# Centring a layer norm by two fp32r products on high and low parts, in place of one float32 product

## The chip, the cores and the metric

One core of a Trainium2 chip runs the whole program. The metric is the device time of one execution in microseconds (us). The kernel before takes 2686.6 us, the median of three runs (2685.15 to 2687.59).

## What is computed

One layer of a hybrid decoder trunk on 2048 tokens of width 1024, all in float32. After an RMS norm and one input projection, three groups of heads work side by side: a convolution module (A), a gated MLP with a spatial mix (B) and a state space model (C). Their outputs are concatenated, projected and added to the input; a squared-ReLU MLP and a final norm follow. The change concerns the layer norm over each head of 64 values, which A applies after its convolution and B to its gate:

```
def head_layernorm(x, g, b, n_heads):
    xf = x.astype(jnp.float32).reshape(*lead, n_heads, -1)
    mu = jnp.mean(xf, axis=-1, keepdims=True)
    xc = xf - mu
    var = jnp.mean(xc * xc, axis=-1, keepdims=True)
    y = (xc * lax.rsqrt(var + EPS)).reshape(*lead, -1)
    return y * g + b
...
ya: h = a_val * sigmoid(a_gate); h = causal_dwconv(h, conv_w, conv_b); h = head_layernorm(h, ln_g, ln_b, A_HEADS); silu(h)
yb: v = head_layernorm(gelu(v), ln_g, ln_b, B_HEADS); mix = einsum("hts,bcshp->bcthp", w, v) + b_s; gelu(u) * mix
```

## The kernel before

The tokens are done in two halves of 1024 (`h`), each in two blocks of 512 (`n`). The first stage, about the first 1010 us, holds input projection and mixers. `ORDER` lists the projection's column tiles of 128: a (A's gate and value), b (B's gate and input), x, z and d (C's), and s, where C's state space part begins. Large products take three fp32r products per tile: operands are split into a high and a low part (`split_w` for weights, `norm1_tr` for activations), and `mm3` (lines 247 to 249) adds high x high, high x low and low x high in one bank of PSUM.

The mixers' work is put between these products by a planner in the program. Each piece is a generator that yields the time at which it wants to go on; a clock per engine (`clk.pe`, `clk.dve`, `clk.act`, `clk.pool`) is advanced by estimates as instructions are written, and `pump`, called after every fourth step of a projection, runs the generators that are due. TensorE's order is the order of writing. The other engines are ordered by a list scheduler that knows priorities (`tc.high_priority`). Every engine runs its own queue strictly in order.

The layer norm is `centred_` (line 520). Channels lie on partitions, tokens on the free axis. For a tile of 128 channels x 512 tokens, four float32 products (line 525) multiply each 128x128 block, as the stationary operand, by the constant matrix `cen`: identity minus 1/64 within each head of 64. That transposes and centres at once, into one bank `pc` of the PSUM ring `ln`, which has two banks and also serves the transpositions `ta` and `tpx` and the spatial mix `pm`. Then ScalarE squares (line 528), VectorE sums over 64 (line 531), GpSimd takes the power -1/2 (`rstd_of`, lines 287 and 288), and VectorE multiplies `pc` by it (line 534), which frees the bank. A transposes the result back (`ta`, line 562); B multiplies it by the spatial weights (`pm`, line 617).

`gen_a` (line 538) runs once per half and a tile: 30 taps on VectorE (line 549, 1024 tokens), then `LAG_A1` = 12000 ns of the planner's time, then `centred` for each block. `gen_b` (line 610) runs once per half, b tile and block, behind the activation that makes the tile `gv` (two buffers). Both have 4 tiles x 2 halves x 2 blocks: 32 calls of `centred`.

The ring `raw` of four tiles of 128x512 (`RAWB`) takes loads of y for the output projection (`load_split`, line 274), which begins after the mixers.

Of the kernel before, what the change touches and what calls it, by code (L numbers as in the profile page):

```python
# [9 lines left out]
F32 = mybir.dt.float32  # L10
F32R = mybir.dt.float32r
# [5 lines left out]
P = 128  # L17
# [4 lines left out]
NB = T // 512  # L22
# [10 lines left out]
RAWB = 4  # L33

EVAC, PRI_S, PRI_L, PRI_X = 600, 60, 150, 300

LAG_S, LAG_A1, LAG_A2, LAG_B1, LAG_B2, LAG_N, LAG_DT, LAG_H = 3000, 12000, 5000, 1000, 5000, 5000, 20000, 4000
# [4 lines left out]
def kernel(  # L42
# [6 lines left out]
    nc = tc.nc  # L49
# [4 lines left out]
    def pool(stack, name, bufs=1, **kw):  # L54
        return stack.enter_context(tc.tile_pool(name=name, bufs=bufs, **kw))
# [9 lines left out]
    const = pool(ctx, "const")  # L65
# [3 lines left out]
    constm = pool(mixers, "constm")  # L69
# [28 lines left out]
    cen = constm.tile([P, P], F32, name="cen")  # L98
    nc.vector.tensor_copy(cen, ident)
    for j in range(2):  # L100
        js = slice(64 * j, 64 * j + 64)
        nc.vector.tensor_scalar_sub(cen[js, js], cen[js, js], 1.0 / 64)
    avg512 = constm.tile([P, 2], F32, name="avg512")
    nc.vector.memset(avg512, 1.0 / 512)
    caw = constm.tile([P, TAPS_A * 4], F32, name="caw")
# [76 lines left out]
    clk = Clk()  # L182
    gens = []

    def V(n, after=0.0):
        clk.dve = max(clk.dve, clk.pe, after) + n / 0.96 + 70
        return clk.dve

    def A(n, after=0.0):
        clk.act = max(clk.act, clk.pe, after) + n / 1.2 + 150  # L190
        return clk.act
# [93 lines left out]
    def rstd_of(ss, n, scale, eps_first=True):  # L285

        nc.gpsimd.tensor_scalar(ss, ss, scale, EPS, op0=ALU.mult, op1=ALU.add)
        nc.gpsimd.tensor_tensor(ss, ss, mhalf[:, 0:n], op=ALU.pow)
        clk.pool += n * 170
        return G(n)  # L290
# [211 lines left out]
    def proj(hT, w, n):  # L502
# [11 lines left out]
        mm3(pairs(), KT)  # L514
        return ps

    def centred(src, name):
        with tc.high_priority(offset=PRI_L):
            return centred_(src, name)

    def centred_(src, name):

        pc = psa.tile([P, 512], F32, tag="ln", name=f"pc_{name}")
        for i in range(4):
            nc.tensor.matmul(pc[:, i * P:(i + 1) * P], src[:, i * P:(i + 1) * P], cen, start=True, stop=True)
        clk.pe += 850
        sq = cv.tile([P, 512], F32, tag="sq", name=f"sq_{name}")
        nc.scalar.activation(sq, pc, AF.Square)
        t = A(512)
        v8 = cv.tile([P, 8], F32, tag="v8", name=f"v8_{name}")  # L530
        nc.vector.reduce_sum(v8, sq.rearrange("p (q e) -> p q e", e=64), axis=mybir.AxisListType.X)
        V(512, t)
        t = rstd_of(v8, 8, 1.0 / 64)
        nc.vector.tensor_mul(sq.rearrange("p (q e) -> p q e", e=64), pc.rearrange("p (q e) -> p q e", e=64),
                             v8.unsqueeze(2).to_broadcast([P, 8, 64]))
        V(512, t)
        return sq
# [3 lines left out]
    def gen_a(h, t, ht):  # L541
        while a_done[0] < 4 * h + t:
            yield clk.pe + 1000
        acc = cv.tile([P, T], F32, tag="aa", name=f"ca_{h}_{t}", bufs=1)
        nc.scalar.activation(acc, ht[:, 0:T], AF.Identity, scale=caw[:, t:t + 1],  # L545
                             bias=vecs[:, CAB + t:CAB + t + 1])
        A(T)
        for k in range(1, TAPS_A):
            nc.vector.scalar_tensor_tensor(acc, ht[:, k:k + T], caw[:, k * 4 + t:k * 4 + t + 1], acc,  # L549
                                           op0=ALU.mult, op1=ALU.add)  # L550
            V(T, clk.act if k == 1 else 0.0)
            if k % 2 == 0:
                yield clk.dve - 3000
        yield clk.dve + LAG_A1
        for n in range(NB):
            xn = centred(acc[:, n * 512:n * 512 + 512], f"a{h}{t}{n}")
            if n == NB - 1:
                a_done[0] += 1
            yield clk.dve + LAG_A2
            tp = psa.tile([P, 512], F32, tag="ln", name=f"ta_{h}_{t}_{n}")  # L560
            for i in range(4):
                nc.tensor.transpose(out=tp[:, i * P:(i + 1) * P], in_=xn[:, i * P:(i + 1) * P], identity=ident)
            clk.pe += 430
            yt = cv.tile([P, 512], F32, tag="yt", name=f"ya_{h}_{t}_{n}")
            nc.scalar.activation(yt, tp, AF.Silu, scale=vecs[:, LAG + t:LAG + t + 1],
                                 bias=vecs[:, LAB + t:LAB + t + 1])
            A(512)
            nc.gpsimd.dma_start(y_d[h][t * P:(t + 1) * P, n * 512:n * 512 + 512], yt)

    def seg_a(h, hT, t):  # L570
# [34 lines left out]
        if h + 1 < NHALF:  # L605
            nc.scalar.copy(halo_a[:, t, :], ht[:, T:T + TAPS_A - 1])
        finish([("u", 0)])
        spawn(gen_a(h, t, ht), ("a", h))

    def gen_b(h, t, n, gv, ug):  # L610
        yield clk.act + LAG_B1
        vn = centred(gv, f"b{h}{t}{n}")
        yield clk.dve + LAG_B2
        pm = psa.tile([P, 512], F32, tag="ln", name="pm")
        for i in range(4):
            for j in range(2):
                nc.tensor.matmul(pm[64 * j:64 * j + 64, i * P:(i + 1) * P],
                                 vn[:, i * P + 64 * j:i * P + 64 * j + 64], wsT[:, 2 * t + j, :],
                                 start=True, stop=True)
        clk.pe += 8 * 142  # L620
        yt = cv.tile([P, 512], F32, tag="yt", name=f"yb_{h}_{t}_{n}")
        nc.vector.scalar_tensor_tensor(yt.rearrange("p (i l) -> p i l", l=P), pm.rearrange("p (i l) -> p i l", l=P),
                                       vecs[:, LBG + t:LBG + t + 1],
                                       bsp[:, t, :].unsqueeze(1).to_broadcast([P, 4, P]),
                                       op0=ALU.mult, op1=ALU.add)
        nc.vector.tensor_mul(yt, yt, ug)
        V(1100)
        nc.gpsimd.dma_start(y_d[h][512 + t * P:512 + (t + 1) * P, n * 512:n * 512 + 512], yt)
# [137 lines left out]
    for h, order in enumerate(ORDER):  # L766
        for st_ in order.split():
            kind, t = st_[0], int(st_[1:])
# [319 lines left out]
    for bi, (h, kb) in enumerate(blocks):  # L1088
# [33 lines left out]
        for nq in range(4):  # L1122
# [11 lines left out]
            for c0 in range(0, NCH, 2):  # L1134
# [15 lines left out]
                acc = accs[h, c0, nq]  # L1150
# [7 lines left out]
                else:  # L1158
                    ps1 = psa.tile([P, 512], F32, tag="mm", name="mmo1")
                    for g, pg in enumerate((ps, ps1)):  # L1160
                        mm3([[(pg[:, j * NQ:(j + 1) * NQ],) + operands(4 * g + k, c0 + j) for j in range(2)]
                             for k in range(4)], 4)
                        for j in range(2):
                            c = c0 + j
# [76 lines left out]
    for n in range(len(seq1)):  # L1241
# [10 lines left out]
        i = n - (NP * NPAIR - LEADX)  # L1252
# [141 lines left out]
    for u in range(LASTP):  # L1394
        q, h, k = seq2[u]
# [9 lines left out]
        if k == 0 and q in (0, 1, 4):  # L1405
            pp, tag = (ps4[0], "mm2") if h else (ps3, "mm")
# [12 lines left out]
    for i, (u, c0) in enumerate(tail):  # L1419
# [4 lines left out]
        q, h, k = seq2[u]  # L1424
# [38 lines left out]
```

## Time and profile before

| what | value |
|---|---|
| median of three runs | 2686.6 us |
| the profiled execution | 2684.8 us, its span on the profile 2683.1 us |
| TensorE busy | 2640.4 us, 98% of the span |
| VectorE, ScalarE, GpSimd busy | 1738.6, 1325.8, 499.2 us |
| share of the span on the chain that ended last | TensorE 91%, DMA 3%, VectorE 2%, ScalarE, GpSimd and issue 1% each |
| TensorE's clock as granted | 0.997 of full over the run |

PE is TensorE and PEld its loads of stationary operands, which run beside products; DVE is VectorE, ACT ScalarE, POOL GpSimd, and SP the queue that issues most loads. The span is what the trace covers; the execution's own time is 1.7 us longer. A busy TensorE is not one at its peak. The views of the trace give, per group of instructions, count, busy time and mean duration, and the idle time before them with what ended it; the chain of waits goes back from the last instruction to whatever released each step.

### The profile page before, as it was taken

The page shows a single profiled execution, that of the slowest core. Times are in us where ns is not written, and L with a number is a line of the kernel's source. Part 1 is how long each engine was busy: PE and PEld are TensorE (multiplying, and loading weights), DVE is VectorE, ACT ScalarE, POOL GpSimd, SP SyncE. Part 2 cuts the span into 40 slices and gives each one's busy share as a digit, 9 for nine tenths or more (in the row PEclk, how much of TensorE's full clock was granted, in tenths as well). Part 3 has the DMA queues.
Part 4 walks back from the last instruction along what each step waited for, and adds up shares of the span by engine and source line. Part 5 has one row for each costly group of instructions (what it writes and reads, how often), then busy time and mean ns, then how long its engine had stood idle before and what let it go on. Part 6 is the DMA issues. An engine that isn't in the chain of part 4 may idle for free.

```text
span 2683.1 us, 38800 instructions
## 1 busy us (share of the span) xinstructions
PE 2640.4 (98%) x14018; PEld 2213.3 (82%) x14018; DVE 1738.6 (65%) x2641; ACT 1325.8 (49%) x2469; POOL 499.2 (19%) x628
## 2 busy tenths in 40 slices
PE   8999999999999999999998999999999999999998
PEld 6788887778878889999997788878887888888887
DVE  6787875496987844664437777787666433555434
ACT  5547673466676534543235455555545433333332
POOL 1013243123333321221052111111111000000001
PEclk9999999999999999999999999999999999999999
DMA  3343443234344226557388666686556645555543
GB/s 121 104 133 117 143 134 99 88 112 137 115 131 133 74 86 223 168 187 241 117 273 271 227 219 207 221 287 219 192 193 213 212 147 157 191 184 177 164 120 124
DMA packets 386897, 446.79 MB, mean 167 GB/s; under 512 B 28301, under 2 KB 279921, under 8 KB 386705
## 3 DMA queue, kind: packets, MB, share of 16 engines
q1 hardware_dynamic: 335520, 314.02, 38.6%
q0 software_dynamic: 28352, 96.62, 9.7%
q10 hardware_dynamic: 22832, 33.68, 3.5%
q8 instruction: 110, 1.80, 0.3%
q14 instruction: 83, 0.67, 0.1%
HBM read 297.28 MB, written 146.93 MB: 166 GB/s over the span
## 4 chain that ended last, share of the span: by engine, by line
PE 91%; DMA 3%; DVE 2%; ACT 1%; issue 1%; POOL 1%; SPq 0%; ACTq 0%; DVEq 0%; POOLq 0%
PE f L1050 14%; PE f L1048 14%; PE f L1049 14%; PE mm L247 10%; PE mm L248 10%; PE mm L249 10%; PE mmo L247 4%; PE mmo L249 4%; PE mmo L248 4%; PE yp L382 1%; PE sp L409 1%; PE op L372 1%; DMA raw_y<-y_d 1%; DMA raw_x<-t_d 1%; DMA raw_x<-h_d 1%
## 5 line engine op out<-in xcount | busy, mean ns | idle before, releaser
L1049 PE MATMUL f<-xlo,w1hi 128*128 128x512 f32 x896 | 352.7, 394 | 3.4 <-DVE xlo L992 3.4
L1048 PE MATMUL f<-xhi,w1hi 128*128 128x512 f32 x896 | 352.7, 394 | 3.0 <-DVE u L1207 3.0
L1050 PE MATMUL f<-xhi,w1lo 128*128 128x512 f32 x896 | 353.0, 394 | 2.6 <-DVE w1lo L1041 2.6
L975 DVE TENSOR_TENSOR falo<-fr,fahi 128x512 fp32r<-128x512 f32 (+1 forms) x237 | 155.3, 655 | 308.1 <-ACT fahi L974 287.7
L1048 PE MATMUL f<-wbhi,fahi 128*128 128x512 f32 x896 | 349.3, 390 | 3.9 <-ACT fahi L1289 3.9
L1050 PE MATMUL f<-wbhi,falo 128*128 128x512 f32 x896 | 349.4, 390 | 0.1
L1049 PE MATMUL f<-wblo,fahi 128*128 128x512 f32 x896 | 349.0, 390 | 0.0
L974 ACT CAST fahi<-fr 128x512 fp32r<-128x512 f32 (+1 forms) x237 | 140.3, 592 | 365.0 <-PE f L1049 360.2
L549 DVE SCALAR_TENSOR_TENSOR ca<-ht,caw,ca 128x1024 f32<-128x1024 f32 x240 | 316.3, 1318 | 5.8 <-ACT ca L545 2.6
L247 PE MATMUL mmo<-whi_o,hi_y 128*128 128x256 f32 x1024 | 294.1, 287 | 4.0 <-DVE x L1166 2.6
L249 PE MATMUL mmo<-whi_o,lo_y 128*128 128x256 f32 x1024 | 288.9, 282 | 0.4 <-DVE lo_y L266 0.4
L248 PE MATMUL mmo<-wlo_o,hi_y 128*128 128x256 f32 x1024 | 288.3, 282 | 0.0
L1050 PEld LDWEIGHTS f<-xhi,w1lo 128*128 128x128 f32 x896 | 169.2, 189 | 42.2 <-DVE w1lo L1041 4.4
L1049 PEld LDWEIGHTS f<-xlo,w1hi 128*128 128x128 f32 x896 | 169.2, 189 | 41.7 <-DVE xlo L992 4.0
L1048 PEld LDWEIGHTS f<-xhi,w1hi 128*128 128x128 f32 x896 | 169.2, 189 | 41.0 <-ACT w1hi L1040 3.4
L1048 PEld LDWEIGHTS f<-wbhi,fahi 128*128 128x128 f32 x896 | 168.6, 188 | 39.4 <-ACT fahi L1289 4.4
L247 PEld LDWEIGHTS mmo<-whi_o,hi_y 128*128 128x128 f32 x1024 | 193.0, 188 | 7.2 <-DVE x L1166 3.7
L1050 PEld LDWEIGHTS f<-wbhi,falo 128*128 128x128 f32 x896 | 168.5, 188 | 35.4 <-DVE falo L1290 0.4
L1049 PEld LDWEIGHTS f<-wblo,fahi 128*128 128x128 f32 x896 | 168.6, 188 | 35.1
L248 PEld LDWEIGHTS mmo<-wlo_o,hi_y 128*128 128x128 f32 x1024 | 193.2, 189 | 1.2 <-issue 1.2
L249 PEld LDWEIGHTS mmo<-whi_o,lo_y 128*128 128x128 f32 x1024 | 192.8, 188 | 0.7 <-DVE lo_y L266 0.6
L247 PE MATMUL mm<-hi_h,whi_x 128*128 128x512 f32 x384 | 159.0, 414 | 0.0
(313 smaller groups left out, 5515.2 us busy)
## 6 DMA issues: line engine op xcount, KB each, us to landing
fr<-f_d SPq DMA_DIRECT2D x208, 256.0 KB, 2.7
w<-in_w_ff_dram SPq DMA_DIRECT2D x176, 256.0 KB, 4.0
f_d<-fs POOLq DMA_DIRECT2D x96, 256.0 KB, 2.8
abc<-acs_d SPq DMA_DIRECT2D x32, 512.0 KB, 4.8
raw_y<-y_d SPq DMA_DIRECT2D x64, 256.0 KB, 4.5
wraw_o<-in_w_out_dram SPq DMA_DIRECT2D x64, 256.0 KB, 4.8
pr_w<-in_w_ff_dram SPq DMA_DIRECT2D x64, 256.0 KB, 5.0
w2t_d<-pr_w POOLq DMA_DIRECT2D x32, 512.0 KB, 4.3
```

The lines of the kernel that those rows point to most:

```text
L247: nc.tensor.matmul(ps, lh, rh, start=(i == 0 and j == 0), stop=False)
L248: nc.tensor.matmul(ps, lh, rl, start=False, stop=False)
L249: nc.tensor.matmul(ps, ll, rh, start=False, stop=(i == n - 1 and j == len(outs) - 1))
L372: nc.tensor.matmul(op[:, i * P:(i + 1) * P], prev[g][:, i * P:(i + 1) * P], xch[:, 5, :], start=True, stop=True)
L382: nc.tensor.matmul(yp[64 * j:64 * j + 64, i * P:(i + 1) * P], xdt[:, hh * 64:hh * 64 + 64], e_t[:, hh, :], start=True, stop=True)
L409: nc.tensor.matmul(sp, w["btok"], w["xdec"], start=True, stop=True)
L549: nc.vector.scalar_tensor_tensor(acc, ht[:, k:k + T], caw[:, k * 4 + t:k * 4 + t + 1], acc, op0=ALU.mult, op1=ALU.add)
L974: nc.scalar.copy(hi, raw)
L975: nc.vector.tensor_sub(lo, raw, hi.bitcast(F32))
L1048: nc.tensor.matmul(ps, lh, rh, start=start and i == 0, stop=False, skip_group_check=True)
L1049: nc.tensor.matmul(ps, lh, rl, start=False, stop=False, skip_group_check=True)
L1050: nc.tensor.matmul(ps, ll, rh, start=False, stop=last, skip_group_check=True)
```

## The change

`cen` is copied once into `cenr`, of type fp32r. A new generator step `cen_split` makes a high part (ScalarE's cast to fp32r) and a low part (VectorE's subtraction) of a 128x512 tile, in two buffers of the ring `raw`; a counter allows two splits that have not been centred yet. `centred_` then issues, for each of four blocks, two fp32r products into the same place of `pc`, one with the high part as the stationary operand and one with the low part. The planner's estimate for the products falls from 850 to 560 ns, and the split's cast and subtraction enter its clocks. A splits its first block behind the taps and its second right behind the first's centring; B splits `gv` as soon as it runs, and its lag counts from VectorE's clock in place of ScalarE's.

```diff
+    cenr = constm.tile([P, P], F32R, name="cenr")
+    nc.vector.tensor_copy(cenr, cen)
...
+    cq = [0]
+
+    def cen_split(src, name):
+
+        while cq[0] >= 2:
+            yield clk.pe + 500
+        cq[0] += 1
+        hi, lo = (const.tile([P, 512], F32R, tag="raw", name=f"c{i}_{name}", bufs=RAWB) for i in "hl")
+        with tc.high_priority(offset=PRI_L):
+            nc.scalar.copy(hi, src)
+            nc.vector.tensor_sub(lo, src, hi.bitcast(F32))
+        A(512)
+        V(512, clk.act)
+        return hi, lo
+
     def centred(src, name):
+        cq[0] -= 1
...
         for i in range(4):
-            nc.tensor.matmul(pc[:, i * P:(i + 1) * P], src[:, i * P:(i + 1) * P], cen, start=True, stop=True)
-        clk.pe += 850
+            for m in range(2):
+                nc.tensor.matmul(pc[:, i * P:(i + 1) * P], src[m][:, i * P:(i + 1) * P], cenr, start=m == 0,
+                                 stop=m == 1)
+        clk.pe += 560
...
+        parts = yield from cen_split(acc[:, 0:512], f"a{h}{t}0")
         yield clk.dve + LAG_A1
         for n in range(NB):
-            xn = centred(acc[:, n * 512:n * 512 + 512], f"a{h}{t}{n}")
+            xn = centred(parts, f"a{h}{t}{n}")
+            if n + 1 < NB:
+                parts = yield from cen_split(acc[:, 512:1024], f"a{h}{t}1")
...
     def gen_b(h, t, n, gv, ug):
-        yield clk.act + LAG_B1
-        vn = centred(gv, f"b{h}{t}{n}")
+        parts = yield from cen_split(gv, f"b{h}{t}{n}")
+        yield clk.dve + LAG_B1
+        vn = centred(parts, f"b{h}{t}{n}")
```

The new clocks move the pieces in every engine's order. Three places follow; a row has the line, the operation and output<-inputs, with the size of the output.

TensorE in the first half, where tile 3 of A (`pc_a`, `ta_3_0`) and tile 2 of B (`pc_b`) are centred, before:

```order
L562 MATMUL ta_3_0_3587<-ident,sq_a_3528 128x128 x4
L525 MATMUL pc_a_3595<-cen,ca_3_3010 128x128 x4
L247 MATMUL mm<-hi_h_4_386,whi_bu_3448 128x512
L248 MATMUL mm<-lo_h_4_387,whi_bu_3448 128x512
...
L249 MATMUL mm<-hi_h_7_413,wlo_bu_3449 128x512
L525 MATMUL pc_b_3619<-cen,gv_2_0_3496 128x128 x4
```

and now (`ch` and `cl` are the high and low parts):

```order
L585 MATMUL ta_3_0_3754<-ident,sq_a_3670 128x128 x4
L544 MATMUL pc_a_3762<-cenr,ch_a_3677 128x128
L544 MATMUL pc_a_3762<-cenr,cl_a_3678 128x128
...
L544 MATMUL pc_a_3762<-cenr,cl_a_3678 128x128
L544 MATMUL pc_b_3778<-cenr,ch_b_3738 128x128
L544 MATMUL pc_b_3778<-cenr,cl_b_3739 128x128
...
L249 MATMUL mm<-hi_h_0_352,whi_bv_3611 128x512
```

Each centring has eight products in place of four. A's second centring and B's next one had 12 projection products between them; now they are adjacent.

VectorE at the same place (`v` the sum of squares, `sq` the final multiply, `wlo` the low part of weights), before:

```order
L531 TENSOR_REDUCE v_a_3530<-sq_a_3528 128x8
L534 TENSOR_TENSOR sq_a_3528<-pc_a_3523,v_a_3530 128x512
L531 TENSOR_REDUCE v_a_3602<-sq_a_3600 128x8
L534 TENSOR_TENSOR sq_a_3600<-pc_a_3595,v_a_3602 128x512
L237 TENSOR_TENSOR wlo_bu_3634<-wraw_bu_0_3635,whi_bu_3633 128x512
L237 TENSOR_TENSOR wlo_bu_3634<-wraw_bu_4_3639,whi_bu_3633 128x512
L531 TENSOR_REDUCE v_b_3626<-sq_b_3624 128x8
L534 TENSOR_TENSOR sq_b_3624<-pc_b_3619,v_b_3626 128x512
```

and now:

```order
L529 TENSOR_TENSOR cl_b_3682<-gv_2_0_3569,ch_b_3681 128x512
L551 TENSOR_REDUCE v_a_3672<-sq_a_3670 128x8
L554 TENSOR_TENSOR sq_a_3670<-pc_a_3661,v_a_3672 128x512
L239 TENSOR_TENSOR wlo_bu_3700<-wraw_bu_0_3701,whi_bu_3699 128x512
L239 TENSOR_TENSOR wlo_bu_3700<-wraw_bu_4_3705,whi_bu_3699 128x512
L529 TENSOR_TENSOR cl_b_3739<-gv_2_1_3609,ch_b_3738 128x512
L551 TENSOR_REDUCE v_b_3733<-sq_b_3731 128x8
L554 TENSOR_TENSOR sq_b_3731<-pc_b_3722,v_b_3733 128x512
L551 TENSOR_REDUCE v_a_3773<-sq_a_3771 128x8
L529 TENSOR_TENSOR cl_b_3908<-gv_3_0_3794,ch_b_3907 128x512
L554 TENSOR_TENSOR sq_a_3771<-pc_a_3762,v_a_3773 128x512
```

A subtraction of a split stands ahead of a sum of squares twice, and once between a sum and its multiply.

SP's queue, which issues the loads: before, the first of four early loads of y stood among weight loads of the first half of the tokens:

```order
L235 DMA wraw_z_0_1262<-in_w_in_dram 128x4x128
L308 DMA abc_2_0_1778<-acs_d_63 128x1024
L274 DMA raw_y_8318<-y_d_57 128x512
L235 DMA wraw_z_4_1266<-in_w_in_dram 128x4x128
L235 DMA wraw_z_0_1339<-in_w_in_dram 128x4x128
```

and now the first loads of y stand at the end of the stage, with the output weights (`wraw_o`):

```order
L237 DMA wraw_z_4_8440<-in_w_in_dram 128x4x128
L878 DMA wraw_o_8650<-in_w_out_dram 128x2x256
L878 DMA wraw_o_8656<-in_w_out_dram 128x2x256
L276 DMA raw_y_8576<-y_d_57 128x512
L276 DMA raw_y_8582<-y_d_57 128x512
L878 DMA wraw_o_8674<-in_w_out_dram 128x2x256
```

All loads of y now follow the splits, which use the same ring.

## Rows read from the trace of the kernel before

**Rows 1.** The page: span, then busy us, share of span, instructions.

```profile
span 2683.1 us, 38800 instructions
...
PE 2640.4 (98%) x14018; PEld 2213.3 (82%) x14018; DVE 1738.6 (65%) x2641; ACT 1325.8 (49%) x2469; POOL 499.2 (19%) x628
```

**Rows 2.** TensorE's waits, 100 to 1010 us: total us, times, longest.

```profile
PE ta L562 <- DVE sq_a L534: 2.2, 2, 1.1
...
PE pc_b L525 <- DVE sq_a L534: 0.8, 1, 0.8
PE pm L617 <- ACT gv L638: 0.7, 1, 0.7
PE pc_b L525 <- DVE sq_b L534: 0.2, 1, 0.2
```

**Rows 3.** Line 525, B's products: count, ns min/median/max, first and last start.

```profile
L525 PE MATMUL pc_b<-cen,gv x128: 270/275/377, 374.1 to 993.4; 128*128 128x128 f32 x128
```

**Rows 4.** The chain of waits, start and us: first and last of six centrings, twice.

```profile
431.19 0.89 PE pc_a L525 x8
...
483.71 0.89 PE pc_b L525 x8
...
949.41 0.89 PE pc_a L525 x8
...
992.55 1.09 PE pc_b L525 x8
```

**Rows 5.** Timeline of products and loads: start, us, engine, line, count at the end.

```profile
84.83 1.85 PE L686 MATMUL td<-sel,dr 128*128 128x16 f32 x16
...
86.50 0.19 PEld L247 LDWEIGHTS mm<-hi_h,whi_x 128*128 128x128 f32 x1
...
86.61 0.19 PEld L248 LDWEIGHTS mm<-lo_h,whi_x 128*128 128x128 f32 x1
...
125.98 1.05 PE L525 MATMUL pc_a<-cen,ca 128*128 128x128 f32 x8
...
126.76 0.19 PEld L247 LDWEIGHTS mm<-hi_h,whi_x 128*128 128x128 f32 x1
```

**Rows 6.** Timeline of output projection's products, 256 columns: first and last of ten.

```profile
1030.05 0.28 PE L249 MATMUL mmo<-whi_o,lo_y 128*128 128x256 f32 x1
...
1031.11 0.28 PE L249 MATMUL mmo<-whi_o,lo_y 128*128 128x256 f32 x1
```

**Rows 7.** Groups by line: a weight split's cast and subtraction, busy us, mean ns.

```profile
L236 ACT CAST whi_z<-wraw_z 128x512 fp32r<-128x512 f32 x32 | 19.2, 617 | 26.5 <-PE mm L248 26.5
...
L237 DVE TENSOR_TENSOR wlo_z<-wraw_z,whi_z 128x512 fp32r<-128x512 f32 x32 | 21.2, 686 | 13.7 <-ACT whi_z L236 12.1 <-DMA xch<-xbc_d 1.7
```

**Rows 8.** Busy us by engine, sum over 100 to 1005 us in four stretches.

```profile
sum 905.00, PE 900.19 PEld 725.85 DVE 676.62 ACT 536.80 POOL 265.76; mean PE 225.05 PEld 181.46 DVE 169.15 ACT 134.20 POOL 66.44
```

**Rows 9.** The chain of waits at the four places where it leaves TensorE.

```profile
436.76 1.29 DVE wlo_bv L237 x2
...
446.77 0.83 ACT L646
...
452.92 1.13 PE pc_b L525 x8
...
746.75 0.62 ACT whi_x L236
...
960.02 0.91 PE pc_a L525 x8
...
964.67 0.70 DVE sq_a L534
```

**Rows 10.** Groups by line: activation-table loads.

```profile
L565 ACT ACT_TABLE_LOAD x14 | 18.0, 1283 | 2.9 <-PE ta L562 2.6
```

**Rows 11.** Loads of y: us to landing; first product on y.

```profile
raw_y<-y_d SPq DMA_DIRECT2D x64, 256.0 KB, 4.5
...
L247 PE MATMUL mmo<-whi_o,hi_y x1024: 278/282/682, 1011.4 to 1426.3; 128*128 128x256 f32 x171
```

## The prediction

> **What bounds the kernel now.** I read the page first: TensorE is busy for 2640.4 of 2683.1 us [rows 1]. Then the list of what TensorE waited for, in the stage that holds the layer norms (100 to 1010 us): four entries at the layer norms and behind them, 2.2 + 0.8 + 0.7 + 0.2 = 3.9 us in all [rows 2]. So TensorE's own work sets the time there, and the change can act in two ways only: by what it takes from or adds to TensorE's stream, or by making TensorE wait. Third, the instructions of line 525: 128 products for B [rows 3], and as many for A. The code has 16 calls of four products for each, so a float32 product is recorded as two, each with a load of its own: eight per call. In the chain of waits a call is worth 0.89 us [rows 4]: 32 x 0.89 = 28.5 us is all that the change can save on.
>
> **What sets the pace of these eight.** Eight records of 128 columns begin at 125.98, and the load behind them at 126.76: 0.10 us each. The 16 records of td, also float32, have only 16 columns; they begin at 84.83, and the load behind them at 86.50: 0.10 us each [rows 5]. An eighth of the columns buys nothing, so the columns don't set this pace. The loads do: every record has a stationary block of its own, and behind td two loads of fp32r operands follow each other at 86.50 and 86.61, with no long product between them yet. A load of an fp32r block takes the same 0.11 us.
>
> **The product, term by term.** Removed: four float32 products, eight loads, 0.89 us. Added: eight fp32r products on the high and low parts, which are stationary and different each time, so eight loads again. No trace of before has an fp32r product of 128 columns. Lower end: fp32r products of 256 columns follow each other every (1031.11 - 1030.05)/9 = 0.118 us [rows 6]; were columns the pace, 128 would take 0.059, a call 0.47, and 32 calls would gain 32 x 0.42 = 13.4 us. Upper end: each fp32r product runs as two records, like the float32 one: 16 x 0.112 = 1.79 us a call, 32 x 0.90 = 28.8 us lost. I take eight loads at 0.112 (28.5/256 = 0.111 per record): 0 us, since the load rows of fp32r are the nearest.
>
> The Trainium skill has a rule for the gain: FP8 and Floating Point Precision, TensorE Precision Notes, gives true FP32 four passes through the array. By that, two fp32r products are two passes, and the change would halve 28.5 us. TensorE: Matmul & The Clock Gate, LDWEIGHTS (loading the stationary operand), has the rule against it: a load costs its columns divided by 1.2 GHz, 107 ns for 128, whatever streams behind it. The loads at 86.50 and 86.61 side with the second, and the sum then keeps its 0.
>
> **The split.** Added per call: a cast on ScalarE and a subtraction on VectorE. The nearest rows, the same shapes in the weight split, are 0.617 and 0.686 us [rows 7]: 32 x 0.617 = 19.7 us on ScalarE, 32 x 0.686 = 22.0 us on VectorE. Over the 905 us of the stage VectorE is busy for 677 and ScalarE for 537 [rows 8]: the sums fit. They are no reason for a loss; queues are. In four places the chain of waits already leaves TensorE at a layer norm and runs through ScalarE, VectorE and GpSimd: around 436, 447, 747 and 961 us [rows 9]. At 446.8 it is the gate's activation, a weight cast, a weight subtraction, the sum of squares, the power on GpSimd (for which VectorE stands), the multiply, and at 452.9 the next centring, which waits for the ln bank that this multiply frees. In the new order VectorE's queue has, in that stretch, a subtraction of a split right ahead of the sum of squares at two calls in a row, and at the next one between the sum and its multiply; and TensorE has two centrings directly behind each other where 12 projection products stood between them. Moreover each split writes into the four-buffer ring raw, so from the third call on it waits for TensorE's centring two calls back, with that multiply queued behind it.
>
> Price: a split on the path costs 0.617 + 0.686 = 1.30 us. Lower end 0: all are covered. Upper end: all 32 on the path, 41.7 us. I take the calls in the two crowded stretches, from 431 to 484 and from 949 to 993 us: six centrings in each [rows 4], about 10 us apart. Of the 12, the last of each stretch has no later call behind it; ten remain, 10 x 1.30 = 13.0 us. The other 20 I cost at nothing: conv tiles are split 12 us of the planner's time before their centring, and elsewhere the projection products between centring and use cover a chain that, from 960.02 to the end of the multiply at 964.67 + 0.70, lasts 5.4 us [rows 9]. Were that cover gone, each would add its 1.30.
>
> **Small terms, all 0.** The copy of the constant matrix: one VectorE instruction, shorter than the 0.69 us of a 128x512 one [rows 7], during the first tiles. Four more activation-table loads (124 for 120 in the order) of 1.28 us [rows 10]: 5.1 us of ScalarE's free time; on the path they would cost that much. The first four loads of y: before, they filled the idle ring early; now SP issues them after the last splits, whose buffers the last centring, at 993 [rows 4], gives back. A load lands in 4.5 us, so by about 998, and the first product on y starts at 1011.4 [rows 11]; if late, 4.5 us once. GpSimd's queue gets nothing. The gate tile gv is freed by the split, earlier than by the centring, and can take away at most the 0.7 us wait for ACT gv [rows 2].
>
> **Sum.** 0 + 13.0. The profiled execution took 2684.8 us, so 2697.8; the median of the runs shown, 2686.6, is 1.8 above it: 2699.6, say 2700.0.
>
> **Rivals.** (1) All splits are covered: no change, 2686.6. For it: TensorE is busy for 900 of the stage's 905 us [rows 8]. Against: the four places of rows 9, with waits already there [rows 2]. (2) Faster: columns, not loads, set the pace of the new products, 0.059 us each, and the splits are covered: 2686.6 - 13.4 = 2673.2. It decides where a record comes in under 0.111 - 5.4/256 = 0.090 us; with the 13.0 us of waits on top even 0.059 gives only 2686.2. Against it: 16-column records at 0.10. The Trainium skill's four passes (FP8 and Floating Point Precision, TensorE Precision Notes) would end here too, at 2686.6 - 14.3 = 2672.3. (3) The change doesn't do what it says: an fp32r product of 128 columns is carried out as two records. 2686.6 + 28.8, plus 0 to 13.0 of waits, of which a slower stream covers some: 2715.4 to 2728.4. For it: no product so short of this type is in the trace; against: those of 256 columns are one record each.
>
> **Numbers.** Forecast 0.64, with a range of its own of 2692 to 2712 (4 to 20 splits on the path, 5.2 to 26); rival 1 0.18, rival 2 0.07, rival 3 0.11. A measurement of this kernel tells 0.2%, 5.4 us, from no change. Faster 0.07, within 0.18, slower 0.75. The range leaves out rival 2, the lower part of rival 1 and the upper two thirds of rival 3, about 0.2: 2685 to 2720.
>
> **What would show it.** Right: 256 records on the new product line, eight per call, still 0.89 us in the chain; casts and subtractions 32 each, near 0.62 and 0.69; TensorE's waits for sq_a, sq_b and the low parts, 2.2 + 0.8 + 0.2 = 3.2 us now, grow by some 13 us, mostly within the two crowded stretches. Wrong on the pace: a call at 0.5 us, or 512 records. Wrong on the queues: waits as before, and the time within 5 us.

## The result and the profile after

The changed kernel takes 2721.2 us (median of four runs, 2719.6 to 2722.0) against 2686.9 for the kernel before on the same chip: 1.0129 times as long, 95% interval 1.0117 to 1.0141. That is 34.3 us more where 13.0 were forecast, and 1.2 us beyond the top of the range. The direction was right, the size was not.

The page of the changed kernel, span and busy times, answers to [rows 1]:

```profile
span 2717.9 us, 38905 instructions
...
PE 2655.3 (98%) x14018; PEld 2225.9 (82%) x14018; DVE 1762.0 (65%) x2674; ACT 1348.1 (50%) x2505; POOL 496.0 (18%) x628
```

TensorE has the same 14018 records as before. The span is 34.8 us longer; TensorE is idle for 62.6 us of it where it was for 42.7, which makes 19.9, and busy for 14.9 more with the same records. VectorE's and ScalarE's additional 23.4 and 22.3 us are mostly the split's 32 subtractions and casts. Each of these is as long as forecast (instructions of lines 528 and 529: ns min/median/max):

```profile
L528 ACT CAST ch_a<-ca x16: 612/620/628, 118.0 to 989.3; 128x512 fp32r<-128x512 f32 x16
...
L529 DVE TENSOR_TENSOR cl_a<-ca,ch_a x16: 674/686/693, 118.7 to 990.0; 128x512 fp32r<-128x512 f32 x16
```

The new product line, 544, has 256 records, 64 in each of four groups (B's high part shown); the loads of one call, from the timeline, begin 0.11 us apart: (130.16 - 129.38)/7 = 0.111, from the second load on.

```profile
L544 PE MATMUL pc_b<-cenr,ch_b x64: 222/274/443, 388.3 to 1030.9; 128*128 128x128 f32 x64
```

```profile
129.38 0.19 PEld L544 LDWEIGHTS pc_a<-cenr,cl_a 128*128 128x128 f32 x1
129.49 0.19 PEld L544 LDWEIGHTS pc_a<-cenr,ch_a 128*128 128x128 f32 x1
...
130.16 0.19 PEld L249 LDWEIGHTS mm<-hi_h,whi_x 128*128 128x128 f32 x1
```

So the products are not where the time went. TensorE's waits between 100 and 1010 us, in total, times and longest, are (compare [rows 2]):

```profile
PE ta L585 <- DVE sq_a L554: 14.5, 5, 4.9
PE pm L641 <- DVE sq_b L554: 5.9, 3, 2.2
PE pc_b L544 <- DVE sq_a L554: 3.6, 1, 3.6
PE pc_a L544 <- DVE sq_b L554: 1.5, 1, 1.5
```

The waits for a multiply of the layer norm (sq_a, sq_b) are 25.5 us where they were 3.2. No entry names the low part `cl`: here the split itself is never what TensorE waits for last. The largest entry, `ta`, belongs to the convolution's tiles and lies outside the crowded stretches of the forecast: its three longest waits are at 153.0, 780.4 and 920.5 us (4.5, 3.5, 4.9 us). The same twelve calls as in these two stretches now run from 454 to 503 and from 988 to 1030 us; 7.1 us of the 25.5 lie there, where 2.0 were before, and some 18 at the 20 other calls, where 1.1 was.

The rest goes with TensorE's clock. Per stretch: us, busy time of each engine, then the granted clock (the column behind POOL), of the changed kernel and then of the kernel before. The stretches are the same in time and not in work, since the changed kernel falls behind:

```profile
370.00:505.00 135.00, 124.36 (x657) 99.77 (x656) 73.67 (x100) 71.20 (x111) 41.83 (x52) 0.97 0.28 87
...
860.00:1030.00 170.00, 161.43 (x844) 131.66 (x843) 108.10 (x138) 84.27 (x131) 47.80 (x51) 0.96 0.27 82
```

```profile
370.00:505.00 135.00, 132.41 (x716) 106.61 (x717) 81.42 (x101) 59.58 (x97) 42.12 (x51) 1.00 0.34 102
...
860.00:1030.00 170.00, 167.84 (x971) 139.47 (x970) 105.56 (x138) 84.51 (x135) 44.60 (x51) 1.00 0.36 113
```

What makes a multiply late shows in the queues ahead of it. VectorE's timeline (start, us, line, operation, count) ahead of the wait at 780 us, at the second block of the second convolution tile of the second half, is:

```profile
766.89 5.43 DVE L569 SCALAR_TENSOR_TENSOR ca<-ht,caw,ca 128x1024 f32<-128x1024 f32 x4
772.23 0.69 DVE L239 TENSOR_TENSOR wlo_x<-wraw_x,whi_x 128x512 fp32r<-128x512 f32 x1
...
775.83 0.68 DVE L551 TENSOR_REDUCE v_a<-sq_a 128x8 f32<-128x512 f32 x1
...
779.53 0.69 DVE L554 TENSOR_TENSOR sq_a<-pc_a,v_a 128x512 f32<-128x512 f32 x1 [1.84 <-POOL v_a L290]
```

The square was ready at 772.5 us, and its sum began at 775.8: four taps `ca` of the next tile (5.43 us) stand ahead, and push the weight subtractions and the convolution steps of C, which stood before the sum already, back behind the square. At the same place of the kernel before no tap stands there, and VectorE even idles before the weight subtraction:

```profile
744.78 0.68 DVE L418 TENSOR_TENSOR prev<-prev,sp 128x512 f32<-128x512 f32 x1
747.40 0.69 DVE L237 TENSOR_TENSOR wlo_x<-wraw_x,whi_x 128x512 fp32r<-128x512 f32 x1 [1.94 <-ACT whi_x L236]
...
751.57 0.68 DVE L531 TENSOR_REDUCE v_a<-sq_a 128x8 f32<-128x512 f32 x1
```

Still, the sum began 2.0 us behind the square there too (749.54 to 751.57), so that VectorE's queue adds 1.3 us at this place. The square itself comes later: ScalarE begins it 2.8 us after the end of the centring's last product, where it was 0.65. An activation-table load and the activation `ya` of the block before now stand ahead of it:

```profile
769.95 1.28 ACT L588 ACT_TABLE_LOAD   x1
771.24 0.79 ACT L588 ACTIVATE ya<-ta,vecs 128x512 f32<-128x512 f32 x1
771.92 0.59 ACT L548 ACTIVATE sq_a<-pc_a 128x512 f32<-128x512 f32 x1
```

and stood behind it:

```profile
748.93 0.61 ACT L528 ACTIVATE sq_a<-pc_a 128x512 f32<-128x512 f32 x1
749.56 1.28 ACT L565 ACT_TABLE_LOAD   x1
```

Ahead of the waits at 153 and 920 us VectorE's queue adds 4.0 and 4.4 us and ScalarE's 2.6 and 3.7. These queues were not only given 32 instructions each; the work that was in them already stands in another order.

### The profile page after: what moved, and what is told of

The parts are those of the page before. It is cut to its first block, busy times and chain, and to the rows that moved or that the text cites. A ratio compares the mean times of both kernels' runs of the same rounds, so it can differ in the third digit from the quotient of the medians.

```text
span 2717.9 us, 38905 instructions
## 1 busy us (share of the span) xinstructions
PE 2655.3 (98%) x14018; PEld 2225.9 (82%) x14018; DVE 1762.0 (65%) x2674; ACT 1348.1 (50%) x2505; POOL 496.0 (18%) x628
## 4 chain that ended last, share of the span: by engine, by line
PE 88%; DVE 6%; DMA 2%; issue 1%; POOL 1%; ACT 1%; DVEq 0%; ACTq 0%; SPq 0%; POOLq 0%
PE f L1074 15%; PE f L1072 15%; PE f L1073 14%; PE mm L249 9%; PE mm L250 8%; PE mm L251 8%; PE mmo L249 4%; PE mmo L251 4%; PE mmo L250 4%; DVE ca L569 2%; PE yp L384 1%; PE sp L411 1%; PE op L374 1%; PE mm L759 1%; POOL v_a L290 0%
```

## The experiments

Ratios are to the kernel before on the same chip, with their 95% interval. The theories at first: **queue** (the split's own instructions make the layer norms late), **order** (the planner's new clocks moved pieces in TensorE's order), **product** (the new products cost TensorE more by themselves).

**e1_products.** The new products alone, the constant with itself in place of the split's parts.

```diff
...
-            nc.tensor.matmul(pc[:, i * P:(i + 1) * P], src[:, i * P:(i + 1) * P], cen, start=True, stop=True)
+            for m in range(2):
+                nc.tensor.matmul(pc[:, i * P:(i + 1) * P], cenr, cenr, start=m == 0, stop=m == 1)
```

> The kernel before with eight fp32r products per centring in place of four float32 ones, in its own order, and no split: every product takes the constant matrix as the stationary operand too, so that the layer norms' values are left out. Product theory (the eight fp32r products cost TensorE more than the four float32 ones): slower by 10 us or more, 2697 or above, records more than 0.112 us apart. Queue theory and order theory both: no change, 2684 to 2690, eight records per call at 0.11 us.

2698.7 us, 1.0046 (1.0031 to 1.0061). The products' loads still begin 0.11 us apart, yet 12.7 us are lost, and three of the four longest waits have no layer norm in them:

```profile
PE ta L565 <- DVE sq_a L537: 4.6, 2, 3.5
PE sp L411 <- DVE cx L378: 2.1, 1, 2.1
PE mm L249 <- ACT zt L758: 1.8, 1, 1.8
PE vp L426 <- POOL sq L403: 1.3, 1, 1.3
```

No theory had said that. The three theories had treated the other engines' order as given.

**e2_split_only.** The split alone, behind the taps and the gate as in the change; its results aren't read.

`split_work` holds the cast and the subtraction of `cen_split`.

```diff
...
+        split_work(acc[:, 0:512], f"a{h}{t}0")
...
+        split_work(gv, f"b{h}{t}{n}")
```

> The kernel before with the 32 casts and 32 subtractions of the split written at the places of the change, but not counted in the planner's clocks; their results are not used, and the float32 products stay. Queue theory (the split's own instructions, in the queues of ScalarE and VectorE, make the layer norms late): most of the 34 us, 2710 to 2721, with TensorE's waits for sq_a and sq_b some 15 us up. Order theory (the planner's new clocks moved the pieces in TensorE's order to where too little stands between a centring and its use): 2687 to 2693.

2688.2 us, 1.0007 (0.9998 to 1.0017). Queue, as it was stated, falls: 64 instructions in the same two queues cost 2.1 us, and no cost at all lies within the interval.

**e3_order_only.** The planner's new clocks, with neither split nor new products.

```diff
-        with tc.high_priority(offset=PRI_L):
-            nc.scalar.copy(hi, src)
-            nc.vector.tensor_sub(lo, src, hi.bitcast(F32))
         A(512)
         V(512, clk.act)
-        return hi, lo
+        return src
...
```

> The changed kernel's planner clocks (560 ns for the products, the split counted on ScalarE's and VectorE's clocks, the limit of two splits, B's lag from VectorE's clock), without the split's instructions and with the float32 products of before: the order alone. Queue theory: 2687 to 2692. Order theory: 2700 to 2721, with waits for sq_a and sq_b of 10 us or more.

2693.6 us, 1.0031 (1.0021 to 1.0040): 7.6 us, a fifth of the loss. The new clocks are worth that much. How much of it is TensorE's own order is not shown, since the other engines' queues moved with it: compared in the traces, 155 of VectorE's 2641 rows and 130 of ScalarE's 2236 lie outside the longest sequence that both kernels have in the same order.

**e5_clocks_before.** The change with the planner's clocks of before: all of its arithmetic in the old order of TensorE.

```diff
-        A(512)
-        V(512, clk.act)
         return hi, lo
...
-        clk.pe += 560
+        clk.pe += 850
...
-        yield clk.dve + LAG_B1
+        yield clk.act + LAG_B1
```

> The change with all its instructions, split and fp32r products, but with the planner's clocks of before: 850 ns for the products, the split not counted, B's lag from ScalarE's clock. Queue theory: as the change, 2712 to 2721. Order theory: near the kernel before, 2687 to 2695. If both act together: between, about 2700.

2700.9 us, 1.0053 (1.0038 to 1.0067), with its longest waits at the same pieces as e1: `sp` for cx, `mm` for zt, `ta` for sq_a (3.5 us), `vp`. Two kernels with different products' operands and one common trait: eight fp32r products a call. Row by row, e1's TensorE order is that of the kernel before apart from these products; but by the same count 230 of VectorE's rows and 114 of ScalarE's stand elsewhere. With e2 it is 46 and 19. A fourth theory: **other engines' order**. The list scheduler that orders VectorE, ScalarE, GpSimd and SyncE sees other products and moves the queues; a queue that was good for 2686 us isn't any more.

**e14_e1_order_kept and e18_e1_order_alone.** Two kernels that exchange the orders. An edge without a semaphore ties each instruction of an engine (`ins`, as written) behind the one that stood ahead of it in another kernel (`steps`, the differences of the places). e14 is e1 with the orders of the kernel before; e18 has four float32 products a call, of the constant with itself, and e1's orders.

```diff
+        for d in steps:
+            at += d
+            if prev is not None:
+                tc.add_manual_dep(ins[at], prev.name, info, reason="order")
+            prev = ins[at]
```

> The eight fp32r products a call of e1_products (they multiply the constant by itself, so the layer norms' results are not the reference's; no split), but every instruction of VectorE, ScalarE, GpSimd and SyncE is tied behind the one that stood ahead of it in the kernel before, so that their orders are those of the kernel before row by row; TensorE's order was that already. Theory 'other engines' order' (e1's +12.7 us is what the list scheduler made of VectorE's, ScalarE's, GpSimd's and SyncE's queues when the products changed): 2686 us, within 3 of the kernel before, and the waits at 374 (sp<-cx), 694 (mm<-zt), 767 (ta<-sq_a) and 919 us (vp<-sq) gone. Theory 'product' (fp32r products on TensorE cost it themselves): 2699 us as e1, and the waits stay.

> The reverse: four float32 products a call as in the kernel before (of the constant with itself, as in e1, so the results are not the reference's), no fp32r product, no split, with the orders of VectorE, ScalarE, GpSimd and SyncE those of e1_products row by row. Theory 'other engines' order': 2699 us (2695 to 2702) as e1, with its waits at 374, 694, 767 and 919 us. Theory 'product': 2686 us as the kernel before.

e14: 2685.5 us, 0.9998 (0.9990 to 1.0007). e18: 2699.9 us, 1.0052 (1.0040 to 1.0065). In the traces no row of VectorE, ScalarE or GpSimd stands elsewhere than in the kernel whose order was taken. The fp32r products cost nothing that these runs can tell, and the order of the other engines costs all of e1's 12.7 us, whichever products run. The waits go with the order; e14's two longest entries, then four of e18's:

```profile
PE ta L565 <- DVE sq_a L537: 2.8, 2, 1.7
PE pm L620 <- DVE sq_b L537: 1.4, 1, 1.4
```

```profile
PE ta L562 <- DVE sq_a L534: 4.7, 2, 3.5
PE sp L409 <- DVE cx L376: 3.0, 2, 2.1
PE mm L247 <- ACT zt L755: 1.8, 1, 1.8
...
PE vp L424 <- POOL sq L401: 1.3, 1, 1.3
```

**e15_e5_order_kept and e17_after_order_kept.** The same edges on VectorE, ScalarE and GpSimd, with the split's instructions left free: e5 in the orders of the kernel before, and the changed kernel in those of e3, which has its TensorE order.

> All of the change's arithmetic with the planner's clocks of before (e5_clocks_before, 2700.9 us), but with VectorE's, ScalarE's and GpSimd's orders those of the kernel before, the split's 32 casts and 32 subtractions put in between by the scheduler; SyncE's is the scheduler's own. Theory 'other engines' order': the time of e2_split_only, 2688 us (2685 to 2691). Theory 'product' or a theory by which the products wait for the split: 2697 to 2702 us.

> The changed kernel (2721 us) with its TensorE order, and with VectorE's, ScalarE's and GpSimd's orders those of e3_order_only (2693.6 us), which has the same TensorE order but no split and float32 products; the split's instructions are put in between. Theory 'other engines' order': e3's time and the split's 2 us, 2696 us (2692 to 2702), so 25 us of the change's 34 gone with no arithmetic changed. Theory 'product' or 'the split's results come late': 2710 us or more.

e15: 2693.5 us, 1.0028 (1.0016 to 1.0039), 7.4 us over the kernel before; e5 was 14.9 over. e17: 2700.4 us, 1.0058 (1.0045 to 1.0072), 14.2 over; the changed kernel is 34.3 over. With the same arithmetic and the same order of TensorE, 20.1 us are gone. Both came out above the forecast, by some 5 us. In e15 TensorE's longest wait is a part of that, and ScalarE's timeline shows it:

```profile
947.72 0.62 ACT L528 CAST ch_a<-ca 128x512 fp32r<-128x512 f32 x1 [11.42 <-DVE ca L567]
948.35 1.28 ACT L660 ACT_TABLE_LOAD   x1
949.64 0.60 ACT L660 ACTIVATE gv<-mm 128x512 f32<-128x512 f32 x1
```

ScalarE idled for 11.42 us at the head of its queue on a cast that waits for VectorE's last tap, with the gate's eviction behind it, for which TensorE stood 2.8 us.

**e22_split_on_vector.** e15 with the cast on VectorE, which makes A's operand (ScalarE makes B's). `_LEFT` names the instructions that the edges leave free.

```diff
-            _LEFT.append(nc.scalar.copy(hi, src).ins.name)
+            _LEFT.append(nc.vector.tensor_copy(hi, src).ins.name)
```

> e15_e5_order_kept with the split's cast on VectorE instead of ScalarE, right ahead of its subtraction, so that no instruction of ScalarE's queue waits for the convolution or the gate; all of the change's arithmetic, the planner's clocks of before. In e15's trace ScalarE idles 11.42 us at 936 to 947.7 us on the cast ch_a, which waits for VectorE's ca, with the eviction gv that TensorE wants queued behind it. Theory 'a cast at the head of ScalarE's queue' (it makes most of e15's 7.4 us): the wait at 950 us (mm<-gv, 2.8 us) and the half clock behind it gone, 2688 us (2685 to 2690); the 32 casts more on VectorE cost nothing where TensorE does not wait for it. Theory 'products wait for both parts' or 'VectorE is full': 2693 us or more, with waits for cl or sq_b.

2689.6 us, 1.0013 (1.0004 to 1.0022), at the upper end of what was expected. The wait for gv is gone, and 4.2 us over the kernel before are left of e15's 7.4; the two intervals overlap. TensorE's longest entries:

```profile
PE pm L639 <- DVE sq_b L552: 4.4, 3, 1.7
PE ta L583 <- DVE sq_a L552: 2.9, 2, 1.8
```

**e19_four_products and e20_high_part_alone.** Half the loads: e14 with four products a call, and the real blocks with the high part alone, cast on VectorE, in the orders of before. The edit of the products in e20, against the changed kernel (e19 has `cenr` for both operands):

```diff
-            for m in range(2):
-                nc.tensor.matmul(pc[:, i * P:(i + 1) * P], src[m][:, i * P:(i + 1) * P], cenr, start=m == 0,
-                                 stop=m == 1)
+            nc.tensor.matmul(pc[:, i * P:(i + 1) * P], src[0][:, i * P:(i + 1) * P], cenr, start=True, stop=True)
```

> e14_e1_order_kept with four fp32r products a call rather than eight (of the constant with itself, so the layer norms' results are not the reference's; no split), the other engines' orders still those of the kernel before. Theory 'loads set the pace' (each product costs its weight load, 0.112 us, float32 or fp32r, two loads for a float32 product): 32 calls x 4 loads x 0.112 = 14.3 us less than the kernel before, 2671 us (2669 to 2676). Theory 'columns or passes set it': 7 us less or nothing (2679 to 2686).

> Real operands with half the loads: the layer norms' blocks cast to fp32r on VectorE, and one fp32r product a block with the exact constant; the low part is left out, so the centring has the cast's rounding. The planner's clocks and the orders of VectorE, ScalarE and GpSimd are those of before, with the 32 casts put in between. Theory 'loads set the pace': 2671 us as e19, and up to 4 more for the casts, 2671 to 2675, faster than both kernels. If the order of the other engines does not fit the shorter calls, waits for sq_a and sq_b eat part: 2676 to 2682 us.

e19: 2673.5 us, 0.9955 (0.9943 to 0.9968), 11.9 us less of the 14.3 that 128 loads are worth. The missing part is in the waits; e14's two entries above, 2.8 and 1.4 us, are larger in e19:

```profile
PE ta L564 <- DVE sq_a L536: 3.7, 2, 2.1
PE pm L619 <- DVE sq_b L536: 3.3, 3, 1.7
```

e20: 2675.3 us, 0.9966 (0.9952 to 0.9979), faster than both kernels, for a centring with the cast's rounding. Of the kernels here that centre the real blocks it is the only one that is.

**e29_e1_next_taps_held, e26_after_next_taps_held, e27_held_and_vector.** Why did the scheduler move the queues? One reason was in sight: the convolution's accumulator `acc` has one buffer. Before, the next tile's taps could not begin until TensorE had centred its second block; now the split frees it. In the changed order 10, 15, 21, 7 and 20 of the next tile's 30 taps stand ahead of this tile's last sum of squares (five of eight tiles), and none before. The edge puts the next tile's first instruction behind that centring's square; e27 also casts on VectorE.

```diff
...
-        nc.scalar.activation(acc, ht[:, 0:T], AF.Identity, scale=caw[:, t:t + 1],
-                             bias=vecs[:, CAB + t:CAB + t + 1])
+        first = nc.scalar.activation(acc, ht[:, 0:T], AF.Identity, scale=caw[:, t:t + 1],
+                                     bias=vecs[:, CAB + t:CAB + t + 1])
+        if "a" in last_sq:
+            tc.add_manual_dep(first.ins, last_sq["a"], no_sync, reason="first tap")
```

> e1_products (2698.7 us; eight fp32r products a call of the constant with itself, so the layer norms' results are not the reference's) with one edge added: the first instruction of the next tile's convolution on ScalarE stands behind the square of this tile's second centring, as the one buffer of the accumulator forced it in the kernel before. In the order of e1 up to 18 of the next tile's 30 taps stand ahead of this tile's last sum of squares on VectorE (8, 14, 18, 7, 14 at five tiles); in the kernel before and with the edge, none. The queues stay otherwise as the list scheduler makes them with eight products. Theory 'accumulator free too early': 2686 to 2690 us, without the waits at 146, 767 and 883 us (ta<-sq_a). Theory 'the scheduler counts longer calls': 2696 to 2700 us, as e1.

> The changed kernel with that one edge and nothing else. In its order up to 21 of the next tile's taps stand ahead of the last sum of squares (10, 15, 21, 7, 20 at five tiles); with the edge none. Theory 'accumulator free too early': the waits ta<-sq_a (14.5 us, longest 4.9) fall to about 3 and the time to 2698 to 2705 us, near e17_after_order_kept (2700.4). Theory 'the scheduler counts longer calls': 2715 us or more.

> The changed kernel with that edge and with the split's cast on VectorE. If the two costs found so far add up (the accumulator's early release, and a cast at the head of ScalarE's queue, worth 4 us between e15 and e22), 2694 to 2699 us, near e3_order_only's 2693.6, which has the same order of TensorE with neither. If VectorE is too full for 32 casts more in this order, 2700 us or more.

e29: 2694.2 us, 1.0042 (1.0030 to 1.0055), against e1's 1.0046. e26: 2716.3 us, 1.0125 (1.0111 to 1.0139), against 1.0129. The theory falls: the waits of A's transpositions went as it said, the time did not. TensorE waits elsewhere instead, for B's layer norms and for the gate (e26):

```profile
PE pm L647 <- DVE sq_b L558: 10.8, 5, 4.6
PE pc_b L548 <- DVE sq_a L558: 3.6, 1, 3.6
PE mm L249 <- ACT gv L668: 3.5, 2, 3.1
...
PE ta L591 <- DVE sq_a L558: 0.2, 1, 0.2
```

e27: 2705.2 us, 1.0082 (1.0068 to 1.0095): the cast on VectorE is worth 11.1 us here, more than the 3.1 between e15 and e22 (33 of VectorE's rows moved with it), but the time stays 6 us above the range expected.

**e30_half_columns_held.** The other reason: eight products of 128 columns count for more in the scheduler than four. e30 is e29 with eight products of 64 columns, so eight loads as ever.

```diff
-                nc.tensor.matmul(pc[:, i * P:(i + 1) * P], cenr, cenr, start=m == 0, stop=m == 1)
+                c0 = 64 * m
+                nc.tensor.matmul(pc[:, i * P + c0:i * P + c0 + 64], cenr, cenr[:, c0:c0 + 64], start=True, stop=True)
```

> e29_e1_next_taps_held (ratio 1.0042 to the kernel before on its chip) with the eight fp32r products of a call cut to 64 columns each, so that they fill the bank as four of 128 do: eight loads a call as before, but half the columns, so a call is no longer for the list scheduler than four float32 products of 128 (still the constant with itself, so the layer norms' results are not the reference's). In its order 36 rows of VectorE differ from the kernel before, where e29 has 90. Theory 'the scheduler counts longer calls': the time falls to within 0.2% of the kernel before, about 2684 to 2690 us, and the waits pm<-sq_b (6.8 us in e29) to 2 or so; the record spacing stays 0.11 us, so a stream of the same length. Theory 'eight products or this type cost TensorE by themselves': 1.003 to 1.005 of the kernel before as e29.

2690.5 us, 1.0011 (1.0002 to 1.0020), where e29 has 1.0042; the intervals don't meet. Its median is a little above the forecast. The wait for sq_b fell from 6.8 to 1.2 us, while `ta`'s for sq_a rose from 0.2 to 3.4. Of VectorE's rows 46 still stand elsewhere, against 135 in e29 (36 and 90 by the count in the expectation). With as many loads, as far apart, halving the columns moved most of these rows back and took most of the loss away. In the e1 line most of the time thus hangs on the columns of a call, by way of the scheduler's orders: a call counts as longer there. The same without the edge was not run.

## Why the prediction was right and wrong

**Right: what bounds the kernel, and the pace.** TensorE's stream sets the time and its waits are what can be added. Eight loads for eight: a call with fp32r products takes what the float32 one took; e14 is 0.7 us from the kernel before, within its interval. Rivals 2 and 3 are out, with 256 records at 0.111 us, and rival 1 by the time itself. e19 gives the other side: half the loads take 11.9 us away. By the Trainium skill, TensorE: Matmul & The Clock Gate, LDWEIGHTS (loading the stationary operand), a load takes its columns divided by 1.2 GHz, an estimate of 107 ns for 128. This case's 0.111 us agrees with it. The Trainium skill, FP8 and Floating Point Precision, TensorE Precision Notes, gives true FP32 four passes. By that, half of the 28.5 us would have come back. No run here shows that gain: every product here has a stationary block of its own.

**Too large: the split's 13.0.** Its presence costs 2.1 us where nothing reads it (e2), and 4.2 (e22, its cast on VectorE) to 7.4 (e15) where the products do and the queues stand as before; in the changed kernel's order of TensorE it is 6.6 (e17 less e3: 14.2 - 7.6). The mechanism, a queue in strict order, was right; the instruction was another one. The forecast named VectorE's subtraction ahead of a sum of squares; what shows in e15 is ScalarE's cast at the head of its queue, waiting for a tap.

**The failed step: "The other 20 I cost at nothing".** Between centring and use, the prediction said, projection products cover a chain of 5.4 us. That chain was read at one place, in the old queues. It was not a long one: behind the centring that starts at 410.1 us the kernel before takes 13.0 us from its end to the end of the multiply, and the next use starts 13.1 us behind that end (ScalarE's timeline, then VectorE's):

```profile
411.29 0.60 ACT L528 ACTIVATE sq_b<-pc_b 128x512 f32<-128x512 f32 x1 [0.35 <-PE pc_b L525]
```

```profile
423.49 0.69 DVE L534 TENSOR_TENSOR sq_b<-pc_b,v_b 128x512 f32<-128x512 f32 x1 [1.83 <-POOL v_b L288]
```

In the new queues other work stands ahead of the square on ScalarE and between the square and its sum on VectorE (at 780 us 2.8 and 3.3 us), and the three longest waits of `ta` are among those 20 calls: some 18 us of waits for a multiply, where the prediction had nothing. In the crowded stretches, for which it had 13.0, these waits grew by 5.1. The prediction used the new order for what the split does to its neighbours and the old one for everything else; the rows that had moved without a split beside them had no term. They are the largest one: after less e17, 34.3 - 14.2 = 20.1 us, and for e1 alone all of 12.7.

**Left out: the clock.** The forecast let a wait cost its own length. TensorE's idle time grew by 19.9 us, and its busy time with the same records by 14.9, which goes with stretches of lower granted clock behind waits (last section).

**Left out: the planner's clocks.** The estimate of 560 for 850 ns, and the split's entries in the clocks, move TensorE's pieces, and the other engines' queues with them. The text told of two centrings behind each other but priced only splits there. e3: 7.6 us, for both together.

**Left out: the early release of `acc`.** Among the small terms the gate tile's earlier release was seen, the accumulator's was not. It moves up to 21 taps; but e26 shows that holding them back alone changes the place of the waits and 0.04% of the time, so it is a missing observation rather than the missing time.

**Sum.** 7.6 (planner) + 6.6 (split) + 20.1 (other engines' order) = 34.3 us, by three differences that share kernels, so each part is worth this only in this sequence. By the intervals they are uncertain by some 2.6, 4.4 and 4.8 us. The first holds moved queues too, and the last also where the split's instructions stand and what SyncE's order does. Of the small terms the y loads and the copy of the constant show nothing. An activation-table load, priced at nothing, does lie on the path at 780 us (1.28 us): one that was there before and changed its place.

**Open.** That the columns of a call move the queues is shown in e1's line, with stand-in operands. For the changed kernel itself it is argued: e17 shows that the order of the other engines is worth 20.1 us, not which of the scheduler's inputs (the longer calls, the split's 64 instructions, the early release) moved which row. A kernel with two products a block, the orders of before on all four queues and the split placed by hand wasn't tried; SyncE's order was never kept in the kernels with a split. From e14 and e22 (2685.5 and 2689.6 us) I estimate 2685 to 2690 us for it, no gain, since its eight loads a call are those of float32.

## What to carry to other kernels

When a list scheduler orders the other engines, an edit on one engine is an edit on all: before pricing it, compare the order on every engine, and look above all at what now stands between the steps of each chain that the bounding engine waits for. To price the edit itself, tie the old order and run it (e14, e17); what is left is the edit, and the rest may be had back. And where each product has its own stationary block, count loads before columns or passes: here 0.111 us each. A cast that waits on one engine's result can hold up evictions at the head of another's queue; moving it to VectorE took 3.1 us (e22, where the intervals overlap) and 11.1 us (e27) away here.

## What the runs showed of the hardware that was not expected

A wait of TensorE can cost a good part of its length again in clock. Windows of the changed kernel around the wait at 776.9 to 780.4 us (us, busy times, then the granted clock):

```profile
780.40:781.50 1.10, 1.10 (x5) 1.10 (x6) 1.10 (x4) 0.95 (x3) 0.12 (x1) 0.50 0.00 0
781.50:785.50 4.00, 4.00 (x10) 3.07 (x10) 4.00 (x7) 4.00 (x11) 0.62 (x1) 0.50 0.58 200
785.50:790.00 4.50, 4.50 (x24) 3.50 (x23) 3.34 (x5) 4.46 (x9) 2.72 (x4) 0.99 0.56 201
```

Behind the wait the clock is granted at 0.50, the lower level of 1.2 GHz, until about 785.5, and 512-column products begin 0.43 us apart instead of 0.23: in 4 us some nine products where there would be seventeen. Up to 1050 us the changed kernel has six such stretches from 100 us on, 34.1 us in all (one of them, and the sum of the six):

```profile
468.17:471.58 3.41, 3.41 (x10) 2.73 (x10) 1.54 (x3) 0.50 (x1) 2.22 (x2) 0.50 0.40 152
...
sum 34.14, PE 28.30 PEld 23.19 DVE 23.24 ACT 13.46 POOL 11.72; mean PE 4.72 PEld 3.87 DVE 3.87 ACT 2.24 POOL 1.95
```

and the kernel before has none between 100 and 1010 us:

```profile
100.00:1010.00 910.00, 905.19 (x4726) 729.91 (x4725) 678.20 (x856) 538.90 (x956) 266.36 (x287) 1.00 0.38 117
```

TensorE is busy for 28.3 us of the six. Had all of that gone at half speed, half of it, 14.2 us, would be time lost: an estimate from these rows, and near the 14.9 us by which TensorE is busy longer with the same records.

The wait's length does not decide it. The stretch at 468.17 stands behind a wait of 1.5 us (`pc_a`, at 466.4). e18 stood at the piece of the wait at 780 us for 3.52 us, and the stretch right behind it ran at the full 2.4 GHz:

```profile
767.70:771.50 3.80, 3.80 (x22) 3.28 (x23) 3.80 (x8) 3.67 (x10) 0.71 (x2) 1.00 0.32 81
```

e1, with that order and a wait of 3.46 us there, ran at 0.52 behind it, and its median is within 1.2 us of e18's all the same. What tells the two apart was not looked for.
